# One unit more in two shares and two longer `early` lists in a hybrid trunk step: two projections per layer leave the attention

## Chip, cores and metric

One Trainium2 chip, one core. The time is device microseconds of one launch of the whole program, two layers and the final norm: 2241.67 us, median of 3 runs (2239.26 to 2246.77).

## What is computed

A context of 128 tokens and 512 latent tokens pass through two layers that share weights. In each layer one input projection feeds three mixers: A, grouped-query attention; B, latent attention with a compressed key; C, a bidirectional RWKV-7 scan. Cut to what matters here:

```python
a_q, a_k, a_v, a_z, b_q, b_ckv, b_kr, b_z, c_in, c_z, gates = _split_in(h @ lp['w_in'])
ya = _block_attention(q, k_all, v_all) * jax.nn.silu(a_z)         # q, k: normalised, rotary
yb = _mla_attend(qb, ckv_all, kr_all, lp) * jax.nn.silu(b_z)      # qb: its rotary part from b_q
yc, _, _ = _branch_c(c_in, s0_f, s0_b, lp)
yc = yc * jax.nn.silu(c_z)
ga, gb, gc = jnp.split(jax.nn.sigmoid(gates), 3, axis=-1)
mixed = ga * (ya @ lp['w_oa']) + gb * (yb @ lp['w_ob']) + gc * (yc @ lp['w_oc'])
xs = xs + gate * (mixed @ lp['w_out'])
```

The 640 tokens lie along the free dimension, channels on the 128 partitions. `h @ w_in` is done in blocks of 128 columns, each named by its number: 18 to 21 are the four query blocks of A, 22 and 23 its key and value, 24 to 27 its z, 28 to 31 the plain and 32, 33 the rotary queries of B, 34 to 37 its z, 38 its compressed key. The gates have 24 blocks of their own.

## The kernel before

**A projection.** `load_w1` (L184) fetches a block of 512 KB in two pieces, ScalarE rounds each (`whi`, L176), VectorE subtracts (`wlo`, L177; in the attention GpSimd does it), two buffers each. `proj_half` (L220) makes 24 matmuls of 128x320 (L227 to L229) into one PSUM bank of tag "f" and yields every two of eight k-tiles, four times; a projection is two halves, 48 matmuls and 8 yields. Its end differs: `raw_cm` (L429) copies the half on ScalarE (L434), `silu2` (L419) takes a tanh on ScalarE and one operation on VectorE (L425, L426), `gate` (L1266) a tanh (L1272) and a DMA to `gsp`. `spill` (L436) puts a `raw_cm` or `silu2` into DRAM (`cmd[w]`); whoever needs block w later asks `cm_tile` (L885), which loads it where (l, w) is in `early` and projects it on the spot otherwise.

**Branch C** runs four scans per layer, p = 0 to 3, one for two heads each, 10 steps long (`c_scan`, L704). Each step consists of four small dependent groups of matmuls (`sca` L771, `scb` L777, `scb` L786, `sca` L790) with copies on ScalarE between them. After three of these groups `pump` (L203) calls the stream of other work, 30 pumps per scan. The stream of scan p is `period(p)` (L1459):

- p below 3: `prepare` for scan p + 1 (`c_prep`, `c_pairs`, and `c_inverse`, a long run of VectorE operations that ends with small matmuls `px`, `py` on TensorE), between them the z projection of branch C and `fb[p]` units, then `share[p+1] - fb[p]` units, then for p below 2 key and receptance for scan p + 2.
- p = 3: the z projection, `at[0]` units, `c_out` of scan 2 (its output), `ctx_e.close()`, which frees the memory of branch C in which the pools of the attention are opened, then `attention_start` (L1206) with `at[1]` to `at[5]` units between its parts: keys and values of A (`a_keys`, L1019; `tok`, L892, transposes into two "f" banks and copies to `kn`, `vn`, L900), queries of pairs 0 and 1. Then the units that are left and the modulations that are left.

A unit is an item of the list `units`: first the spills of `early`, in that order, then gates, as many as fill `sum(share)`: 13 spills and 24 gates, that is, all gates. `fillers(n)` takes the next n from the front; `share[0]` of them run before period 0. Beside them run the modulations (24 in layer 0, 8 in layer 1), one whenever `every = sum(share) / len(mods)` units have passed. The number of yields called at each pump is `rate * (n * 2 * KT / BATCH + 2 * nm + 2) / 30`, with n the projections of the period (its share and 4, 4, 2 or 1 more) and nm its modulations.

**The attention** (L1223) runs eight pairs of heads, i = 0 to 3 for A and 4 to 7 for B. Each has scores, maximum on VectorE (L961), exponential on ScalarE (L963), transposes (L976), a split into two parts (L165, L166) and values (L988, L989). Its stream prepares the next pair: i = 0 to 2 queries and keys, i = 3 to 6 `b_pair`, `b_pair2` and `b_head` for pairs 4 to 7; then `gate_z` (L902) for the z of pair i. `b_pair` (L1135) takes a rotary query block, 32 or 33, for every second pair. `rates[i] / 18` yields are called at each of 18 pumps. Tag "f" has one bank here, two in branch C. At the start of the attention the PSUM pool of branch C is closed and another with tags "pt", "po" and "S" is opened in its banks.

In layer 0 the blocks 22, 24, 25, 27, 32, 33, 35 and 36 are not in `early`; in layer 1 22 is and 37 isn't.

**What sets the order.** The code above gives priorities, not the order. `TileContext(schedule_with_timeline_sim=True)` (L1624) lays the instructions of each engine out by a planner with a timeline of its own, which may pull later instructions forward. On the chip each engine then works in that order.

Of the kernel before, what the change touches and what calls it, by code (L numbers as in the profile page):

```python
# [81 lines left out]


PLAN = [
    dict(share=[7, 5, 5, 7, 13], fb=[0, 0, 3], at=[3, 2, 1, 0, 2, 1], rate=1.0,
         early=[38, 29, 19, 20, 21, 26, 37, 23, 28, 18, 30, 31, 34],
         gates=[1, 0, 0, 0, 0, 1, 1, 0], rates=[8, 8, 22, 30, 21, 16, 25, 13]),
    dict(share=[8, 6, 7, 7, 9], fb=[0, 0, 1], at=[3, 0, 2, 0, 2, 0], rate=0.8,
         early=[26, 38, 18, 19, 30, 29, 22, 23, 28, 21, 20, 31, 34],
         gates=[1, 0, 0, 0, 0, 0, 0, 0], rates=[5, 11, 12, 22, 31, 16, 21, 9]),  # L90
]

# [1549 lines left out]
```

## Time and profile before

| | |
|---|---|
| median of 3 runs | 2241.67 us |
| profiled execution | 2248.71 us |
| its span, first to last instruction | 2246.9 us |
| TensorE (PE) busy | 2095.5 us, 93% |
| VectorE (DVE) busy | 1519.9 us, 68% |
| ScalarE (ACT) busy | 1200.9 us, 53% |
| GpSimd (POOL) busy | 448.1 us, 20% |
| mean granted clock of TensorE | 0.954 |
| layer 0: attention | 746 to 1013 us |
| layer 1: attention | 1821 to 2098 us |

Times within the trace are us from the span's start. A busy time is the union of an engine's instructions; matmuls overlap, so TensorE can be busy and still not at its peak. "<-" behind a bracketed time names who ended the wait. Names such as `pcm` (PSUM tile of a projection), `gt` (gate), `gsl` (spilled block), `qcm` (block to be transposed) are those of the code, with the line that made the instruction.

### The profile page before, as it was taken

How to read it: one execution, taken by the hardware profiler on the slowest of the kernel's cores; microseconds unless marked ns; L12 is line 12 of the kernel's file. 1: busy time of each engine (PE TensorE's matmuls, PEld its weight loads, DVE VectorE, ACT ScalarE, POOL GpSimd, SP SyncE). 2: the span in 40 equal slices, each digit the busy share in tenths (PEclk: the TensorE clock that was granted, in tenths of full speed). 3: DMA queues.
4: the chain of work that ended last, by engine and by line, in shares of the span. 5: the costliest groups of instructions: out<-in, count | busy, mean ns of one | idle time of the engine just before them, and what ended most of it. 6: DMA issues, size and time to landing. Idle time of an engine off the chain costs nothing.

```text
span 2246.9 us, 40407 instructions
## 1 busy us (share of the span) xinstructions
PE 2095.5 (93%) x15380; PEld 1993.5 (89%) x15380; DVE 1519.9 (68%) x2998; ACT 1200.9 (53%) x2734; POOL 448.1 (20%) x618
## 2 busy tenths in 40 slices
PE   8999999999789889999989999999998888899998
PEld 6989999999779768889989999999997777788998
DVE  4676887857645677766647767668575567776673
ACT  4544656556353667762345455555453546776332
POOL 3111223213121221102030012222221231111112
PEclk9998999999799899999999999899896999999999
DMA  6232222232223211036612222222222221111552
GB/s 235 79 96 73 91 81 98 92 101 86 88 83 127 84 39 40 32 103 207 198 54 86 96 76 90 64 91 90 81 91 67 94 85 42 34 48 60 183 186 84
DMA packets 111762, 209.70 MB, mean 93 GB/s; under 512 B 14416, under 2 KB 33488, under 8 KB 111568
## 3 DMA queue, kind: packets, MB, share of 16 engines
q1 hardware_dynamic: 111568, 207.12, 28.5%
q8 instruction: 121, 1.98, 0.4%
q14 instruction: 73, 0.60, 0.1%
HBM read 163.52 MB, written 43.55 MB: 92 GB/s over the span
## 4 chain that ended last, share of the span: by engine, by line
PE 73%; DVE 11%; ACT 8%; issue 3%; DMA 3%; POOL 1%; SPq 0%; DVEq 0%; ACTq 0%; POOLq 0%
PE pcm L227 11%; PE pcm L228 11%; PE pcm L229 11%; PE pA L612 3%; PE sc L958 3%; PE sca L771 3%; PE pm L180 2%; PE pm L182 2%; PE pm L181 2%; PE pp L976 2%; PE scb L786 2%; PE scb L777 2%; PE sca L790 2%; PE pout L180 1%; PE pout L182 1%
## 5 line engine op out<-in xcount | busy, mean ns | idle before, releaser
L227 PE MATMUL pcm<-hh,whi 128*128 128x320 f32 x1952 | 628.0, 322 | 19.6 <-ACT xlo L380 4.6
L229 PE MATMUL pcm<-hh,wlo 128*128 128x320 f32 x1952 | 618.2, 317 | 3.5 <-DVE wlo L177 3.5
L228 PE MATMUL pcm<-hl,whi 128*128 128x320 f32 x1952 | 618.6, 317 | 0.0
L227 PEld LDWEIGHTS pcm<-hh,whi 128*128 128x128 f32 x1952 | 374.9, 192 | 27.6 <-ACT xlo L380 5.1
L229 PEld LDWEIGHTS pcm<-hh,wlo 128*128 128x128 f32 x1952 | 374.1, 192 | 5.4 <-DVE wlo L177 4.2
L228 PEld LDWEIGHTS pcm<-hl,whi 128*128 128x128 f32 x1952 | 374.8, 192 | 1.3
L176 ACT CAST whi<-wraw 128x512 fp32r<-128x512 f32 (+1 forms) x356 | 226.1, 666 | 274.8 <-PE pcm L228 109.7
L177 DVE TENSOR_TENSOR wlo<-wraw,whi 128x512 fp32r<-128x512 f32 (+1 forms) x324 | 248.6, 785 | 119.1 <-ACT whi L176 113.8
L782 POOL COPY ubd<-VZ 64x128 f32<-64x128 f32 x160 | 63.3, 395 | 457.0 <-ACT VZ L779 450.5
L961 DVE TENSOR_REDUCE nm<-sc 128x1 f32<-128x640 f32 x128 | 104.3, 819 | 26.9 <-PE sc L958 25.5
L166 DVE TENSOR_TENSOR pl<-pp,ph 128x512 fp32r<-128x512 f32 x160 | 107.1, 684 | 22.2 <-ACT ph L165 19.4
L182 PE MATMUL pm<-yh,wlo 128*128 128x320 f32 x384 | 118.9, 310 | 0.3 <-DVE wlo L177 0.3
L180 PE MATMUL pm<-yh,whi 128*128 128x320 f32 x384 | 118.8, 309 | 0.0
L181 PE MATMUL pm<-yl,whi 128*128 128x320 f32 x384 | 118.7, 309 | 0.0
L963 ACT ACTIVATE P<-sc,nm 128x640 f32<-128x640 f32 x128 | 102.1, 799 | 25.7 <-DVE nm L961 20.8
L165 ACT CAST ph<-pp 128x512 fp32r<-128x512 f32 x160 | 91.8, 588 | 37.9 <-PE pp L976 20.4
L976 PE MATMUL pp<-small,P 128*128 128x128 f32 x640 | 98.2, 278 | 2.7 <-ACT RB L1004 2.2
L771 PE MATMUL sca<-VZ,L 128*128 128x64 f32 x640 | 91.5, 284 | 1.7 <-DVE VZ L803 1.7
L771 PEld LDWEIGHTS sca<-VZ,L 128*128 128x128 f32 x640 | 89.1, 207 | 3.1 <-DVE VZ L803 2.8
L803 DVE SCALAR_TENSOR_TENSOR VZ<-scb,gm,Zg 64x64 f32<-64x64 f32 x256 | 62.2, 280 | 40.6 <-PE scb L786 33.6
L976 PEld LDWEIGHTS pp<-small,P 128*128 128x128 f32 x640 | 78.0, 143 | 12.8 <-ACT RB L1004 4.3
L612 PE MATMUL pA<-L,BK 128*128 128x128 f32 x640 | 85.5, 276 | 4.0 <-ACT AB L617 3.7
(376 smaller groups left out, 4748.7 us busy)
## 6 DMA issues: line engine op xcount, KB each, us to landing
wraw<-in_win SPq DMA_DIRECT2D x156, 256.0 KB, 3.0
wraw<-in_wg SPq DMA_DIRECT2D x96, 256.0 KB, 3.0
wraw<-in_wmod SPq DMA_DIRECT2D x64, 256.0 KB, 3.0
gsp<-gt SPq DMA_DIRECT2D x48, 320.0 KB, 3.3
gt<-gsp SPq DMA_DIRECT2D x48, 320.0 KB, 3.4
wraw<-in_wo SPq DMA_DIRECT2D x24, 512.0 KB, 4.2
cm<-gsl SPq DMA_DIRECT2D x26, 320.0 KB, 3.4
wraw<-in_wmod SPq DMA_DIRECT2D x16, 512.0 KB, 6.5
```

The source lines that it names most:

```text
L166: self.V.tensor_tensor(out=lo, in0=src, in1=f32(hi), op=ALU.subtract)
L176: self.S.copy(out=hi[part], in_=raw)
L177: sub.tensor_tensor(out=lo[part], in0=raw, in1=f32(hi[part]), op=ALU.subtract)
L180: self.PE.matmul(out, lhsT=lh, rhs=rh, start=first, stop=False)
L181: self.PE.matmul(out, lhsT=lh, rhs=rl, start=False, stop=False)
L182: self.PE.matmul(out, lhsT=ll, rhs=rh, start=False, stop=last)
L227: PE.matmul(p[0:m, 0:H], lhsT=wh[:, kt], rhs=self.hh[:, kt, rs], start=(kt == 0), stop=False)
L228: PE.matmul(p[0:m, 0:H], lhsT=wh[:, kt], rhs=self.hl[:, kt, rs], start=False, stop=False)
L229: PE.matmul(p[0:m, 0:H], lhsT=wl[:, kt], rhs=self.hh[:, kt, rs], start=False, stop=(kt == KT - 1))
L612: PE.matmul(pA[:, j * 128:(j + 1) * 128], lhsT=BK[:, u].rearrange("p a s -> p (a s)"), rhs=L1[h][:, u].rearrange("p a s -> p (a s)"), star ...
L771: PE.matmul(a4[:, d, h], lhsT=L1[h][:, uu[d]].rearrange("p a s -> p (a s)"), rhs=VZ[h][:, cc[d], :], start=(h == 0 and d == 0), stop=False ...
L976: PE.transpose(p[:, qt * 128:(qt + 1) * 128], Ps[qt][:, t * 128:(t + 1) * 128], self.ident)
```

## The change

Only the plan changes. In both layers blocks 32 and 24 are appended to `early`, and `share[3]` and `share[4]` (periods 2 and 3) grow by one each. The list of units is then 15 spills and 24 gates. `gate_z` of pair 0 and `b_pair` of the first pair of B find their block in `early` and load it. The rest of the plan stays; `every` and the yields per pump follow from the sums (`every` 37/24 to 39/24 in layer 0, 37/8 to 39/8 in layer 1).

```diff
-    dict(share=[7, 5, 5, 7, 13], fb=[0, 0, 3], at=[3, 2, 1, 0, 2, 1], rate=1.0,
-         early=[38, 29, 19, 20, 21, 26, 37, 23, 28, 18, 30, 31, 34],
+    dict(share=[7, 5, 5, 8, 14], fb=[0, 0, 3], at=[3, 2, 1, 0, 2, 1], rate=1.0,
+         early=[38, 29, 19, 20, 21, 26, 37, 23, 28, 18, 30, 31, 34, 32, 24],
          gates=[1, 0, 0, 0, 0, 1, 1, 0], rates=[8, 8, 22, 30, 21, 16, 25, 13]),
-    dict(share=[8, 6, 7, 7, 9], fb=[0, 0, 1], at=[3, 0, 2, 0, 2, 0], rate=0.8,
-         early=[26, 38, 18, 19, 30, 29, 22, 23, 28, 21, 20, 31, 34],
+    dict(share=[8, 6, 7, 8, 10], fb=[0, 0, 1], at=[3, 0, 2, 0, 2, 0], rate=0.8,
+         early=[26, 38, 18, 19, 30, 29, 22, 23, 28, 21, 20, 31, 34, 32, 24],
          gates=[1, 0, 0, 0, 0, 0, 0, 0], rates=[5, 11, 12, 22, 31, 16, 21, 9]),
```

## Rows read from the trace of the kernel before

**Rows 1.** busy us (instructions) of each engine by stage; granted clock; DMA share; GB/s

```profile
core 0: us, PE busy (x) PEld busy (x) DVE busy (x) ACT busy (x) POOL busy (x), PEclk, DMA share, GB/s
...
585.00:633.00 48.00, 31.72 (x297) 29.43 (x298) 24.02 (x60) 16.32 (x43) 11.34 (x25) 0.68 0.13 43
...
697.00:746.00 49.00, 43.13 (x327) 41.33 (x325) 24.16 (x58) 18.05 (x40) 10.00 (x7) 0.98 0.40 130
746.00:1013.00 267.00, 242.83 (x1549) 213.05 (x1550) 202.84 (x370) 186.56 (x429) 43.63 (x38) 0.98 0.17 54
...
1698.00:1749.00 51.00, 39.93 (x313) 36.89 (x313) 20.72 (x50) 17.86 (x52) 11.34 (x29) 0.60 0.16 52
...
1775.00:1821.00 46.00, 40.02 (x260) 38.80 (x261) 24.88 (x53) 18.14 (x44) 12.01 (x11) 0.89 0.28 91
1821.00:2098.00 277.00, 248.95 (x1597) 219.58 (x1598) 204.43 (x377) 188.69 (x436) 46.06 (x40) 0.98 0.17 55
```

**Rows 2.** timeline, TensorE: start, us, instruction, in brackets idle before and releaser

```profile
597.59 3.93 PE L683 MATMUL px<-NF,AB 32*32 32x32 f32 x77 [12.66 <-DVE NF L674]
...
1702.77 3.93 PE L683 MATMUL px<-NF,AB 32*32 32x32 f32 x77 [4.09 <-DVE mean L823]
```

**Rows 3.** busy time by stage, behind the inverse of layer 0

```profile
597.00:618.00 21.00, 19.04 (x208) 18.20 (x208) 5.54 (x16) 4.79 (x17) 3.27 (x10) 0.50 0.13 42
```

**Rows 4.** timeline, ScalarE, end of branch C in layer 0

```profile
583.92 0.42 ACT L434 COPY qcm<-pcm 128x320 f32<-128x320 f32 x1
...
626.55 0.75 ACT L900 COPY kn<-pqt 128x512 f32<-128x512 f32 x2
...
633.03 0.44 ACT L1272 ACTIVATE gt<-pcm 128x320 f32<-128x320 f32 x1 [2.28 <-PE pcm L229]
```

**Rows 5.** timeline, TensorE, first matmuls of the attention in both layers

```profile
746.04 1.11 PE L924 MATMUL scc<-KT,QT 128*128 128x128 f32 x4 [0.31 <-DVE modc L254]
...
1820.91 0.63 PE L924 MATMUL scc<-KT,QT 128*128 128x128 f32 x4 [0.41 <-DVE BK L850]
```

**Rows 6.** chain of waits, shares of 747:784, 850:882, 1821:1864, 1924:1956

```profile
by line: DVE rp L871 13.3%; PE sc L958 12.1%; DVE nm L961 12.1%; DVE pl L166 9.0%; PE pp L976 8.1%; ACT P L963 7.8%; issue 4.7%; PE pq L1080 4.3%; DVE QT L166 3.8%; PE pcm L227 3.2%; PE pcm L229 3.2%; PE pcm L228 3.2%; ACT ph L165 3.1%; DVE
...
by line: ACT P L963 10.1%; ACT ph L165 7.1%; issue 6.8%; PE sc L958 6.5%; DVE rp L871 5.8%; ACT QR L1170 5.4%; ACT QR L1169 5.3%; PE pcm L228 4.8%; PE pcm L229 4.3%; ACT QT L168 4.2%; PE pp L976 4.1%; PE pcm L227 4.1%; PE po L989 4.1%; PE p
...
by line: PE sc L958 11.4%; DVE rp L871 10.6%; PE pp L976 8.3%; DMA wraw<-in_win 7.7%; DVE nm L961 7.6%; ACT P L963 6.1%; PE po L989 5.0%; issue 4.4%; ACT ph L165 3.9%; PE po L988 3.2%; POOL wlo L177 2.9%; PE pcm L229 2.8%; PE pcm L228 2.7%;
...
by line: PE pp L976 8.2%; DVE QT L169 8.1%; DVE pl L166 8.0%; PE sc L958 7.5%; PE pcm L227 7.3%; PE po L989 6.9%; PE pcm L229 6.9%; PE pcm L228 6.9%; DVE rp L871 6.2%; DVE nm L961 4.9%; issue 3.9%; PE po L988 2.3%; PE pkr L1132 2.3%; ACT wh
```

**Rows 7.** timeline, TensorE, first and last of a dense run of projections

```profile
563.00 0.31 PE L227 MATMUL pcm<-hh,whi 128*128 128x320 f32 x1
...
564.32 0.31 PE L227 MATMUL pcm<-hh,whi 128*128 128x320 f32 x1
```

**Rows 8.** timeline, VectorE, a subtraction for weights beside the inverse

```profile
585.55 0.69 DVE L177 TENSOR_TENSOR wlo<-wraw,whi 128x512 fp32r<-128x512 f32 x1
```

**Rows 9.** timeline, ScalarE, evictions of gates in the tails of both layers

```profile
703.81 0.43 ACT L1272 ACTIVATE gt<-pcm 128x320 f32<-128x320 f32 x1
...
743.49 0.43 ACT L1272 ACTIVATE gt<-pcm 128x320 f32<-128x320 f32 x1
...
1811.81 0.43 ACT L1272 ACTIVATE gt<-pcm 128x320 f32<-128x320 f32 x1
...
1819.50 0.43 ACT L1272 ACTIVATE gt<-pcm 128x320 f32<-128x320 f32 x1
```

**Rows 10.** busy time of tile pcm alone, pair 7 of both layers

```profile
979.00:1013.00 34.00, 7.56 (x48) 7.04 (x48) 0.96 (x2) 0.88 (x2) 1.00 0.45 150
2059.00:2098.00 39.00, 15.68 (x96) 14.29 (x96) 1.93 (x4) 1.76 (x4) 1.00 0.36 116
```

**Rows 11.** the page, DMA issues: KB each, us to landing

```profile
cm<-gsl SPq DMA_DIRECT2D x26, 320.0 KB, 3.4
```

**Rows 12.** busy time by stage, pair 0 of layer 0

```profile
747.00:784.00 37.00, 32.72 (x188) 29.29 (x187) 30.59 (x50) 25.59 (x61) 8.98 (x7) 0.85 0.18 55
```
## The prediction

> **What bounds the kernel now.** I read the trace in this order: busy time by stage, TensorE's order at the end of branch C, the point at which the attention begins, and the chain of waits inside the attention.
>
> By stage [rows 1], TensorE is the fullest engine, but not evenly. At the end of branch C each layer has a stretch in which it stands still for a third or a fifth of the time: in 585 to 633 it is busy 31.72 of 48.00 us, in 1698 to 1749 39.93 of 51.00, at a low granted clock (0.68 and 0.60). Behind it come the tails, 697 to 746 and 1775 to 1821, then the attention, where TensorE is busy 242.83 of 267.00 and 248.95 of 277.00 us while VectorE and ScalarE have about 75% and 70%. So the attention is mixed: no engine is full, TensorE is nearest.
>
> What the empty stretch is made of is seen in TensorE's order [rows 2]: it stands 12.66 us (layer 0) and 4.09 us (layer 1) until VectorE's inverse for scan 3 is done. After it come small dependent matmuls of scan 3 at clock 0.50 [rows 3], the lower of the two levels, 1.2 GHz; with only these to do, TensorE waits between them too. In layer 0 the projection of the key of A, whose code stands behind the first steps of scan 3, is evicted at 583.92 [rows 4]: the planner pulls forward whatever it can. Then its transposes hold both banks of tag "f" until their copy into `kn` runs at 626.55, and the first gate behind it ends its first half at 633.03. `kn` lies in pools that open when `ctx_e` closes, behind the output of scan 2. I call this copy the barrier. All projections that stand before it in the code (the rest of period 2, then in period 3 the z projection, `at[0]` = 3 units and in layer 0 the key) run ahead of the hole; all behind it run in the tail.
>
> The tail ends when the last unit and the last modulation have: the attention's first matmul, at 746.04, was released by that modulation's `modc`, and in layer 1, at 1820.91, by the output of scan 3, which had stood behind the tail's units [rows 5]. So a unit more in the tail moves the attention's begin.
>
> In the attention the chain of waits [rows 6] changes engine every microsecond or less. The lines of projections have 9.6% of 37 us in pair 0 of layer 0, 13.2% of 32 us in its pair 3, 8.3% of 43 us and 21.1% of 32 us in layer 1.
>
> **The change part by part.** Units 32 (rotary query of B, pairs 0 and 1) and 24 (z of A, pair 0) become the 14th and 15th of the list. By the counts, 7 + 5 units of layer 0 go before period 1, so both are computed beside scan 1; in layer 1, where 8 + 6 go before it, the first falls into period 0. No share there grows, so two gates leave, and each of periods 2 and 3 gets one gate more. All 24 gates are in branch C before and after. Per layer, 96 matmuls therefore leave the attention (48 in pair 0, 48 in pair 3), and in effect 48 go to period 2 and 48 to the tail.
>
> One projection at full flow: nine matmuls from 563.00 to 564.32 [rows 7], 0.147 us each, 48 of them 7.06 us. Four projections, 28.2 us of TensorE's time, change place; none is saved.
>
> *The gate in period 2.* One unit more behind the preparation (five in layer 0, seven in layer 1) pushes z, three gates and in layer 0 the key 7.06 us back. In layer 0 they end at about 591 in place of 583.92, still ahead of 597.59: the 12.66 us hold it whole. In layer 1 the hole is 4.09 us, so some 3 us are left over; they delay the inverse's matmuls or fall between scan 3's. Its two subtractions on VectorE, 0.69 us each [rows 8], go into the queue on which the inverse waits: up to 1.4 us. Against this, the rate at which the stream is called grows (by the formula from 3.67 to 3.93 yields per pump in layer 0, from 2.06 to 2.33 in layer 1), so the output of scan 2 is placed one pump earlier (9th for 10th, 15th for 16th), worth about as much. I take 0 per layer; the ends are -2 (the earlier output alone) and +3 (layer 1's rest alone). If the cover were gone it would cost 7.06.
>
> *The gate in the tail.* Nothing there hides it. In layer 1 the last gate stands 1819.50 - 1811.81 = 7.7 us behind the half before it; in layer 0 the last four, with modulations and transposes, take (743.49 - 703.81) / 4 = 9.9 us each [rows 9]. The modulations are spread thinner but are no more, so I take 7.7; the ends are 7.06 and 9.9. Two layers: +15.4 (14.1 to 19.8).
>
> *What leaves the attention.* On the chain [rows 6] the two projections have 0.096 x 37 + 0.132 x 32 = 7.8 us in layer 0 and 0.083 x 43 + 0.211 x 32 = 10.3 in layer 1: 18.1 us. A second view: pair 7 has one projection in layer 0 (48 matmuls, 34 us) and two in layer 1 (96, 39 us) [rows 10], 5 us for one more, which would give 20 for four; but the two stretches also differ in what follows them. Of what the chain shows, a part can be lost to the next engine; in return the casts, subtractions and evictions of the projections leave too. I take 18.1. The ends are 28.2 (all of it) and 5 (the projections mostly fill time in which the softmax waits anyway).
>
> *Transfers and order.* Each moved projection adds a spill and a load on SP, 320 KB, 3.4 us to landing [rows 11]; the spills take the place of gate spills. The load of z fills a tile that is first needed at the end of pair 0; that of the query replaces 7 us of matmuls. Behind them on SP stand weight loads and outputs of pairs, which are issued ahead. I take 0, and 3.4 per layer where the query's load comes late. In pair 3 the stream has 10 yields at a rate set for 18, so the preparation of pair 4 comes earlier, ahead of the pair's own softmax; its casts `QR` have 10.7% of 32 us of the chain [rows 6], 3.4 us. I take 0, as they only change places, and 3.4 to either side per layer.
>
> The sum: 0 + 15.4 - 18.1 + 0 = -2.7 us. The profiled execution took 2248.71 us, 2246.9 of it the span, so 1.8 lie around it; it is 7.0 above the median of 2241.67. The difference is made in its rows and applied to the median: 2239.0.
>
> **A rule weighed.** The trace has clock 0.50 behind the hole [rows 3], after TensorE stood 12.66 us, and 0.98 over the attention [rows 1]. The Trainium skill, page "TensorE: Matmul & The Clock Gate", section "HAM oscillation — how this bites in real kernels", says that gaps in TensorE's work put its clock back to the low level and that work should be laid so that it never waits long; the trace agrees in the hole. By the rule the change is good there and bad in the attention's first pair, which loses its filler: the third rival.
>
> **The rivals.**
>
> *The attention is bound by TensorE* (faster). For it: TensorE is busy 91% and 90% of the attention [rows 1]. Then 0.9 x 28.2 = 25.4 come back: 15.4 - 25.4 = -10, 2231.7. Against: busy time counts overlapping latency, and the chain shows about two thirds.
>
> *The attention is bound by the softmax chain* (slower). In pairs 0 and 3, maximum, exponential, transposes and splits pass among VectorE, ScalarE and TensorE; projections sit in the gaps. If only a quarter comes back, 7.0, then the tail's 15.4 and 1.5 of the gate in period 2 remain: +10, 2251.6. It decides from the point at which less than 15.4 - 6.7 = 8.7 us of the 28.2 come back: then the kernel is slower by more than 6.7.
>
> *The clock falls in the attention's first pairs* (slower). Pair 0 of layer 0 is at 0.85 already [rows 12] and loses 48 matmuls. TensorE has about a third of its chain [rows 6]; if half of that third ran at 1.2 GHz it would take 6 us more, 12 in two layers: -2.7 + 12 = +9, 2251. Against: the low part of pair 0 follows waits that are there with the projection too.
>
> *The change doesn't reach the hole* (slower). The planner goes by its own times; if it lays period 2's gate behind the barrier, the tails take 14.1 more: +11.4, 2253.1. Against: in both layers all that stood before the barrier ran ahead of it.
>
> **How the numbers follow.** About 0.3%, 6.7 us, is what a measurement of this kernel can tell from no change. The forecast, 2239 with its own range of 2235 to 2248: 0.38. TensorE-bound: 0.34. Softmax-bound: 0.14. Clock: 0.06. Hole missed: 0.08. So faster 0.34, same 0.38, slower 0.28. All favourable ends together would give -25 us, all others +34; they will not fall together. 2225 to 2256 takes in the faster rival with 7 us below it and the slower ones with 3 above.
>
> **What would show it.** Right: TensorE's wait before the inverse's matmuls falls from 12.66 to about 6 us; the copy into `kn` keeps its place, within 3 us, against the start of scan 3; behind it the tail holds 11 gates in layer 0 (10 before) and the attention begins some 8 us later, counted from the barrier; pairs 0 and 3 together are 8 to 10 us shorter per layer. Wrong: a barrier that moves with the gate, a pair 0 as long as before, or a granted clock that falls in the attention. The planner lays out the whole order anew, so shifts of a few us where nothing was changed are the weakest point of this sum.

## The result and the profile after

The changed kernel takes 2267.81 us (median of 4 runs, 2264.98 to 2274.97) beside 2244.22 for the kernel before on the same chip: ratio 1.011, 95% interval 1.008 to 1.014, slower by 23.6 us. The profiled execution has a span of 2267.5 us (before 2246.9).

**Branch C** did what was forecast. Busy time by stage of the kernel after, cut at the points that answer to those of [rows 1]:

```profile
core 0: us, PE busy (x) PEld busy (x) DVE busy (x) ACT busy (x) POOL busy (x), PEclk, DMA share, GB/s
585.00:634.30 49.30, 40.69 (x357) 38.24 (x354) 26.07 (x59) 18.76 (x49) 9.85 (x23) 0.76 0.27 83
697.00:752.50 55.50, 50.96 (x382) 49.10 (x381) 27.49 (x63) 20.69 (x48) 7.83 (x7) 0.99 0.42 137
1707.00:1760.00 53.00, 46.85 (x370) 43.56 (x369) 22.10 (x51) 19.64 (x55) 10.30 (x29) 0.74 0.25 78
1785.00:1839.60 54.60, 48.66 (x327) 47.00 (x326) 27.09 (x57) 21.03 (x52) 10.85 (x11) 0.91 0.30 97
```

The stretch with the hole is filled: in layer 0 TensorE is busy 40.69 of 49.30 us (31.72 of 48.00 before), in layer 1 46.85 of 53.00 (39.93 of 51.00), and the tails are 6.5 and 8.6 us longer. TensorE's order of the kernel after (start, us, instruction, idle before):

```profile
598.95 4.10 PE L683 MATMUL px<-NF,AB 32*32 32x32 f32 x80 [4.98 <-DVE NF L674]
...
752.52 1.11 PE L924 MATMUL scc<-KT,QT 128*128 128x128 f32 x4 [0.31 <-DVE modc L254]
...
1717.51 4.01 PE L683 MATMUL px<-NF,AB 32*32 32x32 f32 x80 [0.92 <-DVE NF L674]
...
1839.58 0.64 PE L924 MATMUL scc<-KT,QT 128*128 128x128 f32 x4
```

TensorE waits 4.98 us ahead of the inverse's matmuls in place of 12.66, and 0.92 in place of 4.09 [rows 2]. The attentions begin at 752.52 and 1839.58 [rows 5]. ScalarE, end of branch C in layer 0:

```profile
585.75 0.43 ACT L1272 ACTIVATE gt<-pcm 128x320 f32<-128x320 f32 x1
...
591.87 0.42 ACT L434 COPY qcm<-pcm 128x320 f32<-128x320 f32 x1
...
598.00 0.42 ACT L434 COPY qcm<-pcm 128x320 f32<-128x320 f32 x1
...
626.88 0.75 ACT L900 COPY kn<-pqt 128x512 f32<-128x512 f32 x2
...
634.31 0.44 ACT L1272 ACTIVATE gt<-pcm 128x320 f32<-128x320 f32 x1 [2.40 <-PE pcm L229]
```

The gate (585.75) and the key of A (591.87, 598.00) now stand where there was nothing; the barrier is at 626.88 (626.55 before) and the first gate behind it at 634.31 (633.03) [rows 4]. Behind it the tail of layer 0 holds 11 gates.

**The attention** did not. It takes 271.5 and 279.9 us, longer than before (267.0 and 277.6), although 96 matmuls have left each:

```profile
752.50:1024.00 271.50, 238.66 (x1453) 206.01 (x1454) 204.29 (x368) 182.50 (x421) 40.78 (x34) 0.94 0.16 51
1839.60:2119.50 279.90, 242.93 (x1507) 209.66 (x1507) 206.61 (x376) 184.45 (x428) 43.57 (x37) 0.96 0.17 53
```

By pair in layer 0, before and, in the second fence, after (same columns; a pair runs from its first context matmul to that of the next):

```profile
746.00:783.80 37.80, 33.48 (x189) 30.06 (x190) 31.50 (x52) 25.66 (x61) 9.25 (x8) 0.84 0.19 60
783.80:816.40 32.60, 27.27 (x174) 23.28 (x173) 25.51 (x47) 21.72 (x53) 8.21 (x6) 1.00 0.17 54
816.40:849.90 33.50, 30.75 (x194) 24.28 (x193) 24.67 (x48) 21.82 (x51) 4.39 (x4) 1.00 0.07 24
849.90:881.60 31.70, 27.61 (x178) 24.03 (x177) 25.62 (x54) 24.58 (x56) 6.28 (x6) 1.00 0.14 46
881.60:915.50 33.90, 32.12 (x221) 29.61 (x220) 24.17 (x41) 25.59 (x61) 4.74 (x4) 1.00 0.11 38
915.50:944.90 29.40, 27.81 (x179) 24.48 (x178) 22.92 (x53) 22.55 (x51) 6.21 (x6) 1.00 0.10 30
944.90:978.60 33.70, 32.56 (x228) 30.49 (x226) 24.54 (x42) 24.64 (x59) 2.28 (x2) 1.00 0.09 30
978.60:1013.00 34.40, 31.23 (x196) 26.82 (x195) 23.91 (x36) 20.01 (x42) 2.29 (x2) 1.00 0.45 148
```

```profile
752.50:787.60 35.10, 27.95 (x145) 22.76 (x146) 27.97 (x51) 24.28 (x57) 6.96 (x6) 0.86 0.17 51
787.60:824.80 37.20, 30.28 (x188) 25.54 (x188) 28.00 (x47) 22.20 (x55) 8.00 (x6) 0.95 0.19 56
824.80:851.40 26.60, 24.25 (x145) 19.91 (x144) 20.08 (x42) 17.94 (x42) 4.94 (x4) 0.87 0.09 29
851.40:886.80 35.40, 30.93 (x181) 26.55 (x180) 31.65 (x64) 26.58 (x63) 3.73 (x4) 0.90 0.08 27
886.80:922.10 35.30, 32.75 (x221) 29.64 (x220) 21.99 (x38) 23.39 (x55) 4.68 (x4) 1.00 0.15 48
922.10:956.90 34.80, 30.54 (x181) 26.67 (x180) 28.28 (x55) 25.88 (x60) 7.94 (x6) 0.90 0.04 14
956.90:990.60 33.70, 32.65 (x227) 30.34 (x226) 23.11 (x40) 23.58 (x58) 2.27 (x2) 1.00 0.10 31
990.60:1024.00 33.40, 29.30 (x178) 24.60 (x177) 23.22 (x35) 18.64 (x37) 2.26 (x2) 1.00 0.47 151
```

Pairs 0, 2 and 7 have 44, 49 and 18 matmuls fewer and are 2.7, 6.9 and 1.0 us shorter: 10.6. But pairs 1, 3, 4 and 5 have 14, 3, 0 and 2 more and are 4.6, 3.7, 1.4 and 5.4 us longer: 15.1. Pairs 0 and 3 together, forecast 8 to 10 us shorter, are 1.0 us longer (0.6 in layer 1). What changed in the longer pairs is the kind of matmul: by the lines of the projections (L227 to L229) the eight pairs have 48, 48, 67, 29, 48, 48, 48, 48 before and 0, 69, 27, 0, 71, 25, 48, 48 after; the planner pulled part of the key of B, and values and keys of the next pairs' heads, forward into the room. The granted clock, 1.00 before in pairs 1 to 7, is 0.87, 0.90 and 0.90 after in pairs 2, 3 and 5, which have 27, 0 and 25 projection matmuls, but also 0.95 in pair 1, which has 69.

An account per layer, from the same trace: 96 matmuls at 0.147 us [rows 7] are 14.1 us less. TensorE's wait (length less busy time) grows from 24.2 to 32.8 us in layer 0 and from 28.1 to 37.0 in layer 1. The time at granted clock 0.50 grows from 12.0 to 33.3 and from 10.2 to 23.8 us (the PEclk column agrees: 0.94 over 271.5 us is 16 us lost, half of 33). At half the clock I count half of such a stretch as lost, an estimate: +10.7 and +6.8. So -14.1 + 8.7 + 10.7 = +5.3 and -14.1 + 8.9 + 6.8 = +1.6, against +4.5 and +2.3 measured.

What ends TensorE's chain now, in pairs 0 and 3 of layer 0 (chain of waits, 753 to 788 and 851 to 887, shares by line):

```profile
by line: DVE nm L961 21.8%; DMA wraw<-in_win 11.8%; issue 7.0%; DVE rp L871 6.3%; DVE pl L166 6.1%; POOL qrb L239 5.6%; ACT P L963 5.4%; PE pp L976 5.0%; PE sc L958 4.3%; PE po L989 4.2%; DVE QT L166 3.9%; DVE qss L882 2.3%; DVE q L1069 2.1
...
by line: PE sc L958 16.7%; PE pp L976 12.5%; ACT P L963 7.2%; DVE rp L871 6.3%; PE po L989 5.7%; issue 5.4%; PE po L988 5.0%; ACT ph L165 4.3%; ACT KHL L165 3.9%; DVE OT L913 2.7%; DVE KHL L166 2.7%; PE pkh L180 2.6%; DVE nm L961 2.5%; PE p
```

In pair 0 the projections' 9.6% [rows 6] are gone, and VectorE's maximum has gone from 12.1% to 21.8%, the load of the next weights to 11.8%. In pair 3 scores and transposes (`sc`, `pp`), TensorE's own links of the softmax chain, have gone from 6.5% and 4.1% to 16.7% and 12.5%; a part of them ran at the low clock (the four matmuls of a score take 1.42 us at 862.78, in a stretch at 0.50, and 0.83 us at 858.10, at 1.00).

### The profile page after: what moved, and what is told of

The parts are those of the page before. It is cut to its first block, busy times and chain, and to the rows that moved or that the text cites. A ratio compares the mean times of both kernels' runs of the same rounds, so it can differ in the third digit from the quotient of the medians.

```text
span 2267.5 us, 40457 instructions
## 1 busy us (share of the span) xinstructions
PE 2117.4 (93%) x15380; PEld 2007.8 (89%) x15380; DVE 1527.1 (67%) x3008; ACT 1196.7 (53%) x2734; POOL 433.9 (19%) x608
## 4 chain that ended last, share of the span: by engine, by line
PE 69%; DVE 13%; ACT 8%; DMA 5%; issue 4%; POOL 1%; SPq 0%; DVEq 0%; ACTq 0%; POOLq 0%
PE pcm L227 11%; PE pcm L228 10%; PE pcm L229 10%; PE pA L612 3%; PE sc L958 3%; PE sca L771 2%; PE pm L182 2%; PE pp L976 2%; PE pm L180 2%; PE pm L181 2%; PE scb L777 2%; PE po L989 2%; DVE wlo L177 1%; PE scb L786 1%; PE px L683 1%
## 5 line engine op out<-in xcount | busy, mean ns | idle before, releaser
L227 PE MATMUL pcm<-hh,whi 128*128 128x320 f32 x1952 | 630.9, 323 | 13.0 <-ACT gt L1272 3.7
L229 PE MATMUL pcm<-hh,wlo 128*128 128x320 f32 x1952 | 621.9, 319 | 3.9 <-DVE wlo L177 3.7
L227 PEld LDWEIGHTS pcm<-hh,whi 128*128 128x128 f32 x1952 | 377.1, 193 | 20.0 <-ACT gt L1272 5.6
L229 PEld LDWEIGHTS pcm<-hh,wlo 128*128 128x128 f32 x1952 | 376.1, 193 | 5.6 <-DVE wlo L177 4.9
L177 DVE TENSOR_TENSOR wlo<-wraw,whi 128x512 fp32r<-128x512 f32 (+1 forms) x334 | 255.8, 782 | 133.1 <-ACT whi L176 128.8
L976 PE MATMUL pp<-small,P 128*128 128x128 f32 x640 | 103.7, 288 | 9.9 <-DVE pl L166 7.0
L612 PE MATMUL pA<-L,BK 128*128 128x128 f32 x640 | 87.1, 278 | 4.9 <-ACT AB L617 1.6
L612 PEld LDWEIGHTS pA<-L,BK 128*128 128x128 f32 x640 | 80.2, 192 | 6.0 <-ACT AB L617 2.0
```

What stands on the lines that cost most here:

```text
L177: sub.tensor_tensor(out=lo[part], in0=raw, in1=f32(hi[part]), op=ALU.subtract)
L227: PE.matmul(p[0:m, 0:H], lhsT=wh[:, kt], rhs=self.hh[:, kt, rs], start=(kt == 0), stop=False)
L229: PE.matmul(p[0:m, 0:H], lhsT=wl[:, kt], rhs=self.hh[:, kt, rs], start=False, stop=(kt == KT - 1))
L612: PE.matmul(pA[:, j * 128:(j + 1) * 128], lhsT=BK[:, u].rearrange("p a s -> p (a s)"), rhs=L1[h][:, u].rearrange("p a s -> p (a s)"), star ...
L976: PE.transpose(p[:, qt * 128:(qt + 1) * 128], Ps[qt][:, t * 128:(t + 1) * 128], self.ident)
```

## The experiments

All runs in one table. C is the stretch up to the attention's first matmul (in layer 1 from the first matmul of scan 0's preparation, L612), "attention" from there to the end of the last pair, "wait" TensorE's idle time in the attention, "low" its time at granted clock 0.50; each as layer 0 / layer 1, us, from one profiled execution. Ratios are to the kernel before on the same chip, with 95% intervals. The kernel before had medians of 2244.2 to 2246.6 in these comparisons, with single runs from 2235 to 2257, so a difference of less than some 5 us between single traces says little. e1, e4, e6 and e9 leave out the results of two projections per layer and read other blocks' spills in their place; e5 and e7 leave them out too and give TensorE other matmuls instead.

| kernel | median | ratio | C | attention | wait | low |
|---|---|---|---|---|---|---|
| before | 2244.2 | 1 | 746.0 / 598.0 | 267.0 / 277.6 | 24 / 28 | 12 / 10 |
| after | 2267.8 | 1.011 [1.008, 1.014] | 752.5 / 606.8 | 271.5 / 279.9 | 33 / 37 | 33 / 24 |
| e1, attention's side alone | 2245.9 | 1.002 [1.000, 1.003] | 742.6 / 592.4 | 273.1 / 278.7 | 38 / 36 | 27 / 27 |
| e2, C's side alone | 2258.2 | 1.006 [1.004, 1.008] | 751.2 / 609.8 | 264.1 / 274.0 | 22 / 25 | 6 / 10 |
| e3, neutral swap | 2235.7 | 0.995 [0.993, 0.997] | 748.1 / 589.2 | 266.7 / 274.3 | 24 / 25 | 10 / 10 |
| e4, e1 with slower pace | 2258.9 | 1.007 [1.004, 1.009] | 745.0 / 598.1 | 276.6 / 278.3 | 34 / 34 | 38 / 31 |
| e5, e1 with dummies | 2240.0 | 0.998 [0.996, 1.000] | 741.9 / 590.2 | 267.1 / 274.8 | 24 / 25 | 10 / 14 |
| e6, e1 with empty yields | 2248.1 | 1.002 [0.999, 1.004] | 741.1 / 586.7 | 274.2 / 280.3 | 38 / 36 | 24 / 31 |
| e7, dummies twice | 2265.1 | 1.009 [1.006, 1.012] | 745.0 / 589.1 | 275.7 / 286.3 | 21 / 23 | 3 / 10 |
| e8, after with dummies | 2267.0 | 1.010 [1.007, 1.013] | 750.0 / 603.0 | 284.1 / 269.4 | 34 / 22 | 31 / 7 |
| e9, late ones removed | 2225.6 | 0.991 [0.988, 0.993] | 749.3 / 588.6 | 262.0 / 266.6 | 28 / 30 | 23 / 10 |
| e10, one late, layer 0 | 2239.6 | 0.998 [0.996, 1.000] | 752.8 / 592.5 | 260.8 / 274.2 | 24 / 26 | 10 / 7 |
| e11, period 2 alone | 2243.8 | 1.000 [0.998, 1.002] | 753.5 / 589.1 | 266.0 / 274.2 | 24 / 25 | 7 / 7 |
| e12, second swap | 2246.3 | 1.000 [0.999, 1.001] | 745.3 / 592.2 | 266.0 / 277.5 | 26 / 29 | 3 / 7 |
| e13, the change with late ones | 2242.1 | 0.998 [0.996, 1.000] | 751.2 / 599.7 | 258.0 / 268.9 | 27 / 31 | 12 / 14 |
| e14, one late per layer | 2241.5 | 0.997 [0.996, 0.999] | 757.5 / 598.1 | 261.6 / 269.8 | 26 / 28 | 7 / 7 |

### The two sides of the change apart

e1, the attention's side alone, on the kernel before:

```diff
+                self.early |= {(l, 24), (l, 32)}
+                self.cmd[24], self.cmd[32] = self.cmd[26], self.cmd[31]
```

> The kernel before with branch C untouched, but blocks 24 and 32 no longer projected in the attention of either layer (their two results are left out; the spills of two other blocks are read in their place). So only the attention's side of the change is there. The forecast's term: the attentions together get 18.1 us shorter, 2226. Theory A (the attention is bound by the softmax chain on VectorE and ScalarE, the projections lay in TensorE's slack): 0 to -3 us, 2241 to 2244. Theory B (with the projections gone the planner lays the remaining preparation worse, or the clock falls in the early pairs, so the attention itself gets longer): +4 to +8 us, 2248 to 2252, the attentions 4 and 2 us longer as in the changed kernel.

In sum nothing came back: ratio 1.002, the attentions 6.1 and 1.1 us longer than before, with waits and low clock as in the changed kernel. The forecast's -18 is refuted at its root, without branch C. Attention windows:

```profile
742.60:1015.70 273.10, 235.58 (x1453) 203.89 (x1454) 200.21 (x368) 181.96 (x421) 39.73 (x34) 0.95 0.16 50
1816.00:2094.70 278.70, 242.85 (x1507) 210.22 (x1507) 206.53 (x376) 184.45 (x428) 43.57 (x37) 0.95 0.17 53
```

By pair it is not that simple. Pairs 0, 3 and 5 of layer 0 in e1:

```profile
742.60:773.90 31.30, 26.30 (x141) 21.32 (x142) 27.11 (x50) 23.17 (x55) 6.83 (x6) 0.89 0.19 55
836.90:877.10 40.20, 34.60 (x217) 30.80 (x216) 30.10 (x63) 28.04 (x66) 3.85 (x5) 0.96 0.10 32
910.70:945.80 35.10, 29.61 (x178) 25.86 (x177) 29.18 (x60) 26.40 (x62) 6.82 (x6) 0.90 0.04 14
```

Pair 0 did give its projection back: it is 6.5 us shorter than before (7.7 and 7.4 in e4 and e6, 2.7 in the changed kernel). Pair 3 is 8.5 us longer, with 217 matmuls for 178, 48 of them projections for 29; pair 5 is 5.7 longer, with no projection for 48. The planner had moved later work forward, and the gain of pair 0 was lost there. In layer 1 pair 0 gave nothing back (below).

e2, C's side alone, on the changed kernel:

```diff
-                    self.early.add((l, w))
+                    if w not in (24, 32):
+                        self.early.add((l, w))
```

> The changed kernel's branch C (shares of 8 and 14, 8 and 10; both projections beside it), but 24 and 32 are projected in the attention again as well, from their spills. Only branch C's side of the change is there. If the forecast's C terms are right and C and the attention add: +15 us, 2259, with the attentions of the length that they had before. If the longer attention of the changed kernel comes from how the attention is entered (clock, order) and not from what left it: +22 us, 2266, with pairs 1, 3 and 5 longer here as well.

+13.6 us, and the attentions are not longer (264.1 and 274.0): how the attention is entered does not lengthen it. What lengthened it came with the projections' leaving, be it the gaps or the order that the planner then lays. The sides alone sum to +1.3 + 13.6 = 14.9, the change took +23.6; of the 8.7 between them the runs name no cause, and the swap of e3 alone moved as much.

### What a new layout alone does

e3 and e12 keep the work and swap two neighbours of `early` (e3: 34 ahead of 31 in both layers; e12: 31 ahead of 30 and of 20):

```diff
-         early=[38, 29, 19, 20, 21, 26, 37, 23, 28, 18, 30, 31, 34],
+         early=[38, 29, 19, 20, 21, 26, 37, 23, 28, 18, 30, 34, 31],
```

> The kernel before with the last two blocks of the list in each layer swapped (34 ahead of 31): the same work, the same number of units in each period, but the planner lays the order out anew. It measures what a new layout alone is worth. Theory of a mere layout effect: several us either way, up to the 7 us by which the changed attentions got longer. Otherwise within 2 us of before, 2242 to 2246.

> A second control of a mere new layout: the kernel before with two other neighbours of the list swapped (31 ahead of 30 in layer 0, 31 ahead of 20 in layer 1), the same work in the same periods. The first such swap was 9 us faster than before. If layouts scatter by that much: within 10 us of before to either side, branch C of layer 1 anywhere between 586 and 598 us, the attentions 264 to 268 and 274 to 278 us long. If the first was an outlier: within 2 us of before.

e3 is 8.9 us faster than before, e12 the same. So the planner's new layout alone is worth up to 0.4% of the median here, more than the 0.3% that I took for the measurement; the attentions keep their length in both within 3.3 us. The 7 us by which the attentions grew would be within that scatter of the total. But all four kernels in which pairs 0 and 3 lost their projections and got nothing for them (after, e1, e4, e6) have attentions of 271 to 277 and 278 to 280 us, the others with the work of before 264 to 267 and 269 to 278, but for layer 0 of e8. In layer 1 the two groups all but touch.

### Pace, empty yields, dummies

e4 is e1 with `rates[3]` lowered from 30 to 17 and from 22 to 12:

> As the run with the attention's side alone, and the pace of pair 3 is lowered to the units that are left in it (30 to 17 in layer 0, 22 to 12 in layer 1), so that the preparation is spread over the pair as it was before. If the old pace, now too fast for what is left, crowds the preparation at the start of pair 3 and costs there: 4 to 8 us below the run with the old pace, pairs 3 to 5 shorter. If the softmax chain or the clock sets the pairs: within 2 us of it.

Slower by 13 us than e1, which neither alternative named: a pace too fast for what was left is not the cause.

e5 puts into `cm_tile` (L885), for blocks 24 and 32 of e1, matmuls that nobody reads; e6 puts `yield` alone there; e7 doubles the matmuls; e8 is e5's edit on the changed kernel:

```diff
             self.nc.sync.dma_start(out=dst, in_=self.cmd[w])
+            if w in (24, 32):
+                for half in range(2):
+                    p = ps.tile([128, 512], F32, tag="f", name="pdum")
+                    rs = slice(half * H, half * H + H)
+                    for kt in range(KT):
+                        for a in (self.hh, self.hl, self.hh):
+                            self.PE.matmul(p[:, 0:H], lhsT=self.hl[:, kt, 0:128], rhs=a[:, kt, rs], start=True, stop=True)
+                        if kt % BATCH == BATCH - 1:
+                            yield
```

> The run with the attention's side alone, and where the projections of 24 and 32 stood the stream gives the same 48 matmuls of 128x320 each, on data that lies in SBUF, into a bank that nobody reads (so the results of 24 and 32 are left out): TensorE's work and the number of yields are as before, the weight loads, casts, subtractions and evictions are gone. Clock theory (without its fillers TensorE waits, its clock falls, and this eats the gain): the low stretches of the attention vanish, the attentions take 264 to 267 and 274 to 278 us, TensorE's waits fall back to some 24 us per layer, total 2238 to 2245. Casts and evictions were the price of the projections: 5 us or more below before, under 2239. Order theory (the loss is the planner's order of what is left, whatever TensorE does beside it): 271 and 279 us as with the projections gone.

> As the run with the dummies, but the stream only yields eight times at each place and issues nothing: the rest of the preparation is placed in the code as before, no matmuls. Order theory: the attention gets shorter than before, by up to the 14 us per layer that left (253 and 264 us), total under 2235. Clock theory: no better than with the projections gone, 270 to 275 and 277 to 281 us, low stretches in pairs 0 to 3, total 2242 to 2250.

Attention windows of e5, then of e6:

```profile
741.90:1009.00 267.10, 243.38 (x1549) 212.58 (x1550) 199.63 (x368) 181.64 (x421) 39.00 (x34) 0.98 0.16 52
1807.50:2082.30 274.80, 249.84 (x1601) 221.21 (x1602) 203.76 (x375) 184.57 (x428) 41.55 (x36) 0.98 0.17 54
```

```profile
741.10:1015.30 274.20, 235.70 (x1453) 202.54 (x1454) 200.34 (x368) 181.70 (x421) 39.77 (x34) 0.96 0.16 50
1813.40:2093.70 280.30, 243.92 (x1507) 211.10 (x1507) 207.21 (x376) 184.64 (x428) 44.21 (x37) 0.95 0.17 53
```

With 96 useless matmuls per layer the attention is 7.1 and 5.5 us shorter than with empty yields in their place, and the whole kernel 8.1 us faster (2240.0 against 2248.1). The wait falls by 14.8 and 11.4 us, about the 14.1 that the dummies take: they fit into it almost whole. The time at the low clock falls from 24 to 10 and from 31 to 14 us, which by the estimate above is worth 6.8 and 8.5. The expectation that the low stretches vanish was too strong: they fall to the level of before. The casts, subtractions and evictions, gone in e5, had cost the attentions 0 and 3 us; the whole, 4.3 faster than before, can't be told from no change. Two limits: 8.1 us is no more than the swap of e3 gave. And the dummies bring back the planner's order as well: pairs 4 to 7 of layer 0 have 48, 48, 48 and 48 projection matmuls in e5, as before, and 48, 0, 72 and 24 in e6. So these two runs do not part the filled gaps from the order.

> As the run with the dummies, with 96 matmuls in place of 48 at each of the two places of a layer: TensorE gets 14.1 us more per layer than before. It measures what a matmul costs in pairs 0 and 3. TensorE-bound there: +14 us per layer against the run with the dummies, +28 in all. Slack (the softmax chain sets the pairs): under +6 per layer. In between it gives the share of a projection that the attention feels.

```profile
745.00:1020.70 275.70, 255.06 (x1645) 224.14 (x1646) 200.64 (x368) 182.39 (x421) 39.08 (x34) 0.99 0.16 50
1820.20:2106.50 286.30, 263.52 (x1699) 233.88 (x1699) 202.25 (x376) 184.50 (x428) 41.72 (x37) 0.98 0.16 52
```

The second 96 cost 8.6 and 11.5 us of their 14.1, 25 us in the medians. So the attention stands at a kink: what is added costs most of its time, what is taken from pairs 0 and 3 returns, in total, none.

> The changed kernel with the 48 dummy matmuls at the two places in the attention of each layer from which the projections left. Clock theory: the attentions take 264 to 267 and 274 to 278 us as in the run with only branch C changed, total 2256 to 2262, some 8 us faster than the changed kernel although TensorE does 28 us more. Without an effect of the clock: 10 us or more slower than the changed kernel, 2278 or over.

This one missed. 28 us of matmuls more did cost nothing (2267.0 against 2267.8), but the 8 us of gain stayed out. The attention of layer 1 is 10.5 us shorter than in the changed kernel, that of layer 0 is 12.6 longer. Its pairs 2 to 4:

```profile
817.60:856.60 39.00, 35.80 (x234) 29.72 (x233) 24.93 (x49) 22.45 (x53) 3.91 (x4) 1.00 0.11 31
856.60:893.00 36.40, 31.38 (x185) 27.67 (x184) 27.63 (x58) 23.84 (x58) 3.92 (x4) 0.86 0.10 34
893.00:931.40 38.40, 35.05 (x217) 31.39 (x216) 23.05 (x38) 24.73 (x59) 4.80 (x4) 0.91 0.11 34
```

The planner crowded 95 projection and dummy matmuls into pair 2 and left 25 in pair 3 and 5 in pair 5; pair 3 stands at clock 0.86. Pair 3 fits the pattern of few projections and a low clock; pair 4, at 0.91 with 67 of them, does not. Why the planner laid it so stays open.

### The same number taken from the late pairs

e9 is e1 with other blocks:

```diff
-                self.early |= {(l, 24), (l, 32)}
+                self.early |= {(l, 36), (l, 37 if l else 35)}
```

> As the run with the attention's side alone, but the two projections that leave the attention of each layer are the z of the last pairs (35 and 36 in layer 0, 36 and 37 in layer 1; their results are left out) and 24 and 32 stay. In pairs 4 to 7 of the kernel before TensorE waits only 1 to 3 us per pair, against 3 to 9 in pairs 0 to 3. If what a projection is worth depends on TensorE's slack in its pair: the attentions get 7 to 14 us shorter per layer than before, total 2218 to 2232. If the softmax chain and the clock hold the late pairs as they hold the early ones: 0 to +7 per layer, 2244 to 2255, with low clock stretches in pairs 4 to 7.

2225.6 us, 20.3 faster than before, where the same number of matmuls out of the early pairs returned nothing. The attentions are 5.0 and 11.0 us shorter (7 to 14 each were expected). Attention windows of e9, then its pair 7 in both layers, and in the second fence pair 7 of layer 1 before:

```profile
749.30:1011.30 262.00, 234.10 (x1453) 202.82 (x1454) 200.99 (x366) 182.26 (x421) 39.65 (x34) 0.96 0.17 54
1810.70:2077.30 266.60, 237.04 (x1507) 206.47 (x1507) 201.04 (x374) 185.08 (x428) 42.07 (x37) 0.98 0.18 57
979.80:1011.30 31.50, 26.99 (x136) 21.72 (x135) 19.88 (x30) 17.04 (x37) 3.39 (x2) 0.84 0.26 83
2047.20:2077.30 30.10, 25.57 (x148) 21.15 (x147) 20.89 (x32) 17.07 (x37) 2.25 (x2) 0.94 0.27 86
```

```profile
2059.30:2098.50 39.20, 37.15 (x244) 33.81 (x243) 24.58 (x38) 20.52 (x44) 2.29 (x2) 1.00 0.36 120
```

In layer 1 pair 7 had 96 projection matmuls, waited 39.20 - 37.15 = 2.0 us and is 9.1 us shorter without them; in layer 0 (34.4 before) 2.9. There too the clock falls where no projection is left (0.84 and 0.94): even late ones are not returned whole.

The 16 traces together point the same way. Of the pairs behind pair 0 with more than 30 projection or dummy matmuls, 24 of 181 have any time at clock 0.50, 0.6 us in the mean; of those with 30 or fewer, 32 of 43, 3.8 us in the mean; many of these pairs recur almost unchanged from kernel to kernel, so they are fewer cases than they seem. By place, the mean length of pair 0 is 36.1 us with one projection and 31.7 with none in layer 0, but 39.7 and 40.0 in layer 1; of pair 3 in layer 1 it is 32.0 and 35.1; of pair 7, both layers, 38.7 with two, 34.8 with one and 29.7 with none. One projection is worth 4 to 5 us in pair 7, 4 in pair 0 of layer 0 and nothing in pair 0 of layer 1; pair 3 without one is longer, not shorter, since other work is put there.

### What branch C's unit costs, and versions that are faster

e11 is the unit of period 2 alone: the last two entries of `share` are 8, 13 and 8, 9, block 24 comes as a 14th spill and is still projected in the attention:

> Only the unit in period 2, in both layers: block 24 is projected beside branch C as a 14th spill and still projected in the attention too, periods 3 and the attention as before. The prediction says 0 per layer (-2 to +3): 2240 to 2250. If the hole doesn't take it: +7 per layer, 2258.

2243.8 us, ratio 1.000: free, as forecast. Its layer 0 looks less clean:

```profile
603.27 3.93 PE L683 MATMUL px<-NF,AB 32*32 32x32 f32 x77 [6.13 <-DVE NF L674]
...
632.10 0.76 ACT L900 COPY kn<-pqt 128x512 f32<-128x512 f32 x2
```

The wait before `px` falls to 6.13 us, but `px` itself (603.27 for 597.59) and the barrier (632.10 for 626.55) come 5.6 us later, and the attention begins at 753.5. In the changed kernel with the same unit `px` stood at 598.95. So the hole takes the unit, and whether scan 3 starts as early as before hangs on the layout; one trace doesn't settle it.

e10 is this in layer 0 alone with block 36 in place of 24 and gone from the attention; e14 does it in both layers (36, 37); e13 is the whole change with 36 and 35, 36 and 37 in place of 32 and 24:

```diff
-         early=[38, 29, 19, 20, 21, 26, 37, 23, 28, 18, 30, 31, 34, 32, 24],
+         early=[38, 29, 19, 20, 21, 26, 37, 23, 28, 18, 30, 31, 34, 36, 35],
```

> A candidate on the kernel before: in layer 0 alone one unit more in period 2, and the projection that leaves the attention is 36 (z of pair 6), from the late pairs; layer 1 as before. By the prediction's terms: the hole of 12.66 us takes the gate for 0 to 3 us, the attention of layer 0 gets up to 7 us shorter if TensorE is the bound there: 2237 to 2244. If the late pairs have slack as well: 2244 to 2250.

> A candidate: one unit more in period 2 of both layers (0 us in the run with that alone), and one late projection per layer leaves the attention (36 in layer 0, 37 in layer 1). By the runs so far each is worth some 5 us: 2232 to 2238. If it is no better than the candidate for layer 0 alone, or a mere layout's worth: 2238 to 2246.

> The same change, one block exchanged for another: the two projections of a layer that go beside branch C are 36 and 35 in layer 0, 36 and 37 in layer 1, in place of 32 and 24; shares as in the changed kernel. If place in the attention decides and the parts add: branch C +14 (the run with C's side alone) and the attentions -16 to -20 (the run with the late ones removed): 2238 to 2246, some 22 to 28 us faster than the changed kernel. If more than the place of the projections is wrong with the change: 2252 or over.

e13 is 25.7 us faster than the changed kernel and 4.5 faster than before, with the same shares: the choice of the blocks made the loss. e10 and e14 gain 6.3 and 5.2 us, less than a mere swap gave in e3, and e10's interval takes in no change; e14 comes out at the second of its two expectations, since its second layer adds nothing to e10 (its C is 757.5 and 598.1 us). None beats e3, the swap of two list entries, at 2235.7, 32 us below the changed kernel: the fastest here with all the work in it.

## Why the prediction was wrong

Forecast 2239, range 2225 to 2256; measured 2267.8.

- **The hole: right.** The wait before `px` fell to 4.98 us (about 6 named), the barrier moved 0.3 us (within 3 named), layer 0's tail has 11 gates, the attention begins 6.2 us later counted from the barrier (some 8 named), and period 2's unit alone cost nothing (e11).
- **The gate in the tail: right, a little low.** +15.4 forecast; the attention of layer 0 begins 6.5 us later and layer 1's C is 8.8 us longer, 15.3. The 598.0 us of layer 1's C is at the top of what nine kernels with an untouched branch C show (mean 744.9 / 591.6, up to 598.1). Against their mean, the four with all of the change in C (751.2 / 604.8) take 6.3 + 13.2 = 19.5, inside the ends given (with the 0 of period 2's gate).
- **What leaves the attention: wrong, and the whole miss.** -18.1 forecast, +6.8 in the trace, 25 us; alone, without branch C, +7.2 in the attentions and nothing in the total (e1). Three steps failed. The share of the projections on the chain was read as what comes back; but it says only who ended last while they were there. Without them the maximum, the next weights and TensorE's own softmax links ended as late. The second view, 5 us for one more projection in pair 7 [rows 10], was right for pair 7 (e9) and carried over to pairs 0 and 3, where TensorE waited 3 to 9 us per pair already. And the planner's order was put at 0, on the ground that the casts that come earlier "only change places": work did change places, and pair 3 became 3.7 and 4.3 us longer without its projection. The lower end, a return of 5 us, left out that it could be negative.
- **The rivals.** The softmax-bound one had the place and the direction (+10), the clock one the rest (+9). They were priced as alternatives; in the traces they come together: without the projections TensorE waits longer and spends more time at the low clock (wait +8.7 and +8.9 us, low clock +21.3 and +13.6). That the waits bring the low clock about is likely but not shown by itself. Their two prices together, +10 and the clock's 12, would have been the +22 of the traces (15.3 + 6.8), which may be luck, since no run parts the two. The likeliest rival, TensorE-bound, was wrong for pairs 0 and 3 and nearer for the late pairs, where 16 of 28.2 us came back (e9). The hole took its gate, so the last rival fell away. The argument against the clock rival, that the low stretch of pair 0 follows waits that are there with the projection too, held for pair 0 (12.0 us low before, 9.5 after) and said nothing of pairs 1, 2, 3 and 5.
- **The rule weighed.** The section "HAM oscillation — how this bites in real kernels" of the Trainium skill's page "TensorE: Matmul & The Clock Gate" wants work laid so that TensorE never waits long. The traces agree with its direction, not with the place that the prediction drew from it: the attention's first pair had no more low clock than before (9.5 us for 12.0 in layer 0, 10.2 for 10.2 in layer 1), and the low stretches appeared in later pairs, in 32 of the 43 that were short of projections.
- **Transfers and order at 0.** The loads of the two spills were not tried by themselves. The pace was (e4: 13 us lost). That the planner's layout alone moves the total by up to 9 us (e3) was named as the weakest point and not put into the range.

What stays open: how the attention's loss divides between the clock, the waits and the planner's order, which all change together when a projection leaves, and the 8.7 us by which the whole change costs more than its two sides.

## What to carry to other kernels

Before filler work is moved off a stage, read the engine's wait per part of the stage. Where it waits much already (3.5 to 8.8 us in pairs 0 and 3, for a filler of 7.06), taking the filler away can buy waiting in place of time. Take it from the parts where the engine waits least: the same edit with blocks of pairs 5 to 7 was 25.7 us faster than with blocks of pairs 0 and 3. Where a planner lays the order, see also what it moves into the room: in e1 one pair got 6.5 us shorter, and two later ones 14.2 longer. And a forecast of 0.1% can't be tested where two swapped list entries move a planner's layout by 0.4%.

## What was not expected of the hardware

Matmuls whose result nobody reads made the attention faster: 192 of them, 28 us of TensorE's time, for 12.6 us less in the attentions and 8.1 in the total (e5 against e6; the planner's order differs too), while the next 192 cost 25 us (e7). Behind pair 0 the granted clock fell to 0.50, the level of 1.2 GHz, in 32 of 43 pairs with few or no projections, and in 24 of 181 others: how full TensorE looks over the attention (88% busy after, 91% before, in layer 0) told less of where its clock would fall than the kind of work left in each pair.
